# A diffusion backbone layer on one core: four staging tiles, branch tiles loaded in the output projection, late low parts, down-projection operands staged ahead, modulation weights in eight loads

## The chip, the cores and the metric

The kernel runs on one core of one Trainium2 chip. Each core has five engines that are programmed apart and meet by semaphores: TensorE (PE, with its weight loads shown as PEld), VectorE (DVE), ScalarE (ACT), GpSimd (POOL) and SyncE (SP), which here issues the transfers between the chip's main memory and the on-chip SBUF. Matrix products land in a second on-chip memory, PSUM. The metric is device time in microseconds of one execution. Lower is better.

## The reference

One layer over 2048 latent tokens of 1024 channels, with 256 context tokens ahead of them, all in 32-bit floats. What matters of it:

```python
mx = (silu(c) @ ada_w + ada_b).reshape(b, 1, 6, 1024)       # six modulation vectors
hx = rmsnorm(x, norm1_g) * (1 + mx[:, :, 1]) + mx[:, :, 0]
ux = hx @ w_in                                              # 1024 -> 5120
ox = hgrn_bidir(...)                                        # gated recurrence, 4 heads of 128
y_a = fourier_mix(ux[..., :512]) @ w_a                      # 2-D DFT over positions and channels
y_b = hgrn_readout(ux, ox) @ w_b
yx = (sigmoid(ux[..., GA]) * y_a + sigmoid(ux[..., GB]) * y_b) @ w_out
x = x + mx[:, :, 2] * yx
h2 = rmsnorm(x, norm2_g) * (1 + mx[:, :, 4]) + mx[:, :, 3]
z = depthwise_conv_3x3(h2 @ ffn_up) + ffn_conv_b            # 1024 -> 5632, grid of 32 x 64
x = x + mx[:, :, 5] * ((silu(z[..., :2816]) * z[..., 2816:]) @ ffn_down)
return rmsnorm(x, final_g)
```

## The kernel before

**Products in two parts.** An operand is split into a high part (`hi`, rounded to the format that the matrix product reads) and a low part (`lo = raw - hi`), and a product is three matmuls: hi x hi, hi x lo, lo x hi (`mm3`, L140). `load_split` (L105) loads a raw block of 128 x 512 into a staging tile `rw` (two of them per pool), ScalarE copies it to `hi` (L102), and GpSimd, or VectorE where it is named, subtracts for `lo` (L103). The staging tile is free after the subtraction.

**Order.** The program's text is not the order of issue. The build traces it, and a planner places each engine's instructions by dependences, tile slots and a model of times, with earlier text ahead where both are ready. `tc.issue_after(ins)` holds what is traced inside it behind `ins` on the engine of `ins`, without a wait for its end. Each engine, and SP's queue of transfers, then runs its list strictly in order.

**Stages, in order of time.** `startup` (L277) loads the first two modulation vectors' weights (`ada_w`, 1024 x 2048) as sixteen blocks of 128 x 1024, alternating halves, with the first tokens after the fifth block; it also loads six short vectors as rows (`vec_rows`, L258) on SP's queue, and the weights of the Fourier channels. The products of phase 1 follow: input projection, Fourier mix and recurrence.

Phase 2 (L840) goes over four blocks of 512 tokens. For each, `branches` (L862) loads eight branch tiles `y` (four of the Fourier branch, four of the recurrence) and goes over eight columns `j`: two weight blocks (`wab`), two gate tiles (`gt`, four slots), two products of twelve matmuls into `pj` (two slots), two gate products on VectorE (L895), their sum (L896), and the split into `mh` and `ml`. Between the columns it steps `bg`, a generator that normalizes, transposes and splits the previous block for the feed-forward part (`h2_block`, L934; for the third block `reload_steps`, L951, which reloads the block from memory piece by piece as `xc`). `out_proj` (L902) then multiplies by `w_out` in two halves `c` of 512 columns, eight steps `k` of twelve matmuls each.

Phase 3 (L977) makes 44 tiles of the up-projection `z`. For each, ScalarE applies the centre tap (L997) and the tap below (`be`, L999), VectorE the other seven (L1027), GpSimd adds `be` (L1003); each pair is gated (L1012) and stored to `dZ`.

`down` (L1030) makes eight groups `gi`: two column halves by four token blocks. A group is 22 steps `k` of twelve matmuls: operand `g` from `dZ`, weight `wd` from `ffn_down` (loaded in the groups 0 and 4, kept for the others). After each group four tiles are evicted: times the modulation `m5` (L1095), plus `x` (L1096), squares on ScalarE (L1098); in the second half the inverse root (`rsqrt`, L117), the scaling of a whole row of 1024 (L1107) and the store (L1108).

## Time and profile before

| | us |
|---|---|
| median of three runs | 3155.86 (3153.78 to 3157.29) |
| profiled execution, its own time | 3159.88 |
| its span, first to last instruction | 3158.1 |
| TensorE matmul busy | 3081.7 (98%) |
| TensorE weight load busy | 2556.2 (81%) |
| VectorE busy | 1742.6 (55%) |
| GpSimd busy | 949.1 (30%) |
| ScalarE busy | 930.7 (29%) |

The profile is that of one execution. The share of an engine is an average over stages with different limits, so the stages are read one by one. A matmul's recorded end is modelled, and successive matmuls overlap; the distance from start to start, that is, the length of a stretch over the count of its matmuls, says how fast they go. "PEclk" is the share of its full clock that TensorE was granted. Lines of the kernel are given as L and a number.

### The profile page before, as it was taken

The page shows a single profiled execution, that of the slowest core. Times are in us where ns is not written, and L with a number is a line of the kernel's source. Part 1 is how long each engine was busy: PE and PEld are TensorE (multiplying, and loading weights), DVE is VectorE, ACT ScalarE, POOL GpSimd, SP SyncE. Part 2 cuts the span into 40 slices and gives each one's busy share as a digit, 9 for nine tenths or more (in the row PEclk, how much of TensorE's full clock was granted, in tenths as well). Part 3 has the DMA queues.
Part 4 walks back from the last instruction along what each step waited for, and adds up shares of the span by engine and source line. Part 5 has one row for each costly group of instructions (what it writes and reads, how often), then busy time and mean ns, then how long its engine had stood idle before and what let it go on. Part 6 is the DMA issues. An engine that isn't in the chain of part 4 may idle for free.

```text
span 3158.1 us, 38963 instructions
## 1 busy us (share of the span) xinstructions
PE 3081.7 (98%) x14955; PEld 2556.2 (81%) x14955; DVE 1742.6 (55%) x2493; ACT 930.7 (29%) x1498; POOL 949.1 (30%) x563
## 2 busy tenths in 40 slices
PE   7999999999999999999999999999999998999998
PEld 4977788888888888777877888888888887788786
DVE  6355533566666640366665777777777777111324
ACT  4322111233333331233433222222222223223322
POOL 2200110000000010343443444344444345444543
PEclk9999999999999999999999999999999999999999
DMA  6255644433223232656552111111111113545643
GB/s 245 86 164 185 196 153 150 139 107 105 91 95 112 99 108 74 206 171 209 175 181 68 54 60 50 41 54 47 54 54 34 54 54 114 173 132 168 204 149 132
DMA packets 283051, 374.70 MB, mean 119 GB/s; under 512 B 20701, under 2 KB 158833, under 8 KB 279537
## 3 DMA queue, kind: packets, MB, share of 16 engines
q1 hardware_dynamic: 282865, 372.21, 36.0%
q8 instruction: 118, 1.93, 0.2%
q14 instruction: 68, 0.56, 0.1%
HBM read 270.68 MB, written 101.45 MB: 118 GB/s over the span
## 4 chain that ended last, share of the span: by engine, by line
PE 83%; DMA 6%; DVE 4%; POOL 2%; issue 2%; ACT 2%; SPq 0%; ACTq 0%; DVEq 0%; POOLq 0%
PE z L146 10%; PE z L144 10%; PE z L145 10%; PE pj L144 9%; PE pj L146 9%; PE pj L145 9%; PE dn L1079 4%; PE dn L1078 4%; PE dn L1077 4%; PE pa L782 4%; PE wo L925 1%; PE wo L926 1%; PE wo L924 1%; DMA rw<-in_ffn_down_dram 1%; PE kv L654 1%
## 5 line engine op out<-in xcount | busy, mean ns | idle before, releaser
L1027 DVE SCALAR_TENSOR_TENSOR ac<-z,cw,ac 128x1953 f32<-128x1953 f32 (+2 forms) x308 | 700.8, 2275 | 253.2 <-ACT be L999 242.1
L145 PE MATMUL z<-h,w_up 128*128 128x512 f32 x1408 | 548.0, 389 | 0.0
L146 PE MATMUL z<-h,w_up 128*128 128x512 f32 x1408 | 548.0, 389 | 0.0
L144 PE MATMUL z<-h,w_up 128*128 128x512 f32 x1408 | 547.9, 389 | 0.0
L1003 POOL TENSOR_TENSOR ac<-ac,be 128x1984 f32<-128x1984 f32 x44 | 196.8, 4472 | 427.1 <-DVE ac L1027 413.9
L103 POOL TENSOR_TENSOR gl<-rw,gh 128x512 fp32r<-128x512 f32 x176 | 233.0, 1327 | 274.5 <-ACT gh L102 265.5
L145 PEld LDWEIGHTS z<-h,w_up 128*128 128x128 f32 x1408 | 264.3, 188 | 54.9
L146 PEld LDWEIGHTS z<-h,w_up 128*128 128x128 f32 x1408 | 264.3, 188 | 54.8
L144 PEld LDWEIGHTS z<-h,w_up 128*128 128x128 f32 x1408 | 264.3, 188 | 54.6
L1079 PE MATMUL dn<-wd,gl 128*128 128x512 f32 x704 | 279.8, 397 | 6.2 <-POOL gl L103 5.9
L1077 PE MATMUL dn<-wd,gh 128*128 128x512 f32 x704 | 278.9, 396 | 6.0 <-ACT gh L102 5.8
L1078 PE MATMUL dn<-wd,gh 128*128 128x512 f32 x704 | 278.5, 396 | 0.0
L997 ACT ACTIVATE ac<-z,vt,cw 128x2048 f32<-128x2048 f32 x44 | 90.9, 2066 | 636.4 <-PE z L146 636.4
L102 ACT CAST gh<-rw 128x512 fp32r<-128x512 f32 x176 | 108.8, 620 | 304.2 <-PE dn L1078 206.8
L488 ACT ACTIVATE ev<-pj 128x512 f32<-128x512 f32 (+1 forms) x136 | 79.6, 585 | 367.0 <-PE pj L146 343.3
L1079 PEld LDWEIGHTS dn<-wd,gl 128*128 128x128 f32 x704 | 133.0, 189 | 41.2 <-POOL gl L103 10.4
L1077 PEld LDWEIGHTS dn<-wd,gh 128*128 128x128 f32 x704 | 133.2, 189 | 38.1 <-ACT gh L102 7.1
L1095 DVE TENSOR_TENSOR dtmp<-dn,m 128x512 f32<-128x512 f32 x32 | 21.4, 684 | 249.3 <-PE dn L1079 249.3
L1078 PEld LDWEIGHTS dn<-wd,gh 128*128 128x128 f32 x704 | 133.0, 189 | 31.1
L103 POOL TENSOR_TENSOR w_up<-rw,w_up 128x512 fp32r<-128x512 f32 x88 | 112.8, 1306 | 90.3 <-ACT w_up L102 90.3
L782 PEld LDWEIGHTS pa<-bQ,bkc 128*128 128x128 f32 x896 | 120.7, 191 | 17.0 <-issue 10.5
L782 PE MATMUL pa<-bQ,bkc 128*128 128x128 f32 x896 | 127.5, 286 | 1.3
(310 smaller groups left out, 6193.0 us busy)
## 6 DMA issues: line engine op xcount, KB each, us to landing
rw<-dZ SPq DMA_DIRECT2D x176, 256.0 KB, 3.0
rw<-in_ffn_up_dram SPq DMA_DIRECT2D x88, 256.0 KB, 3.4
dZ<-ac SPq DMA_DIRECT2D x22, 1024.0 KB, 4.4
rw<-in_w_in_dram SPq DMA_DIRECT2D x72, 256.0 KB, 3.2
maw<-in_ada_w_dram SPq DMA_DIRECT2D x64, 256.0 KB, 3.2
rw<-in_w_out_dram SPq DMA_DIRECT2D x64, 256.0 KB, 3.2
x<-dX SPq DMA_DIRECT2D x48, 256.0 KB, 4.9
rw<-in_ffn_down_dram SPq DMA_DIRECT2D x44, 256.0 KB, 3.2
```

Of the source, the lines that this page charges most:

```text
L102: self.nc.scalar.copy(hi, raw)
L103: (eng or self.nc.gpsimd).tensor_tensor(lo, raw, hi, op=SUB)
L144: self.nc.tensor.matmul(ps, lh, rh, start=start and i == 0, stop=False)
L145: self.nc.tensor.matmul(ps, lh, rl, start=False, stop=False)
L146: mm = self.nc.tensor.matmul(ps, ll, rh, start=False, stop=stop and i == last)
L782: mm = nc.tensor.matmul(pa[:, c], kc[:, c], fap(Q, w * P, [(2 * m, nw), (W + m, 2), (1, m)]), start=True, stop=True)
L997: nc.scalar.activation(ac, z, AF.Identity, scale=self.cw[:, 4, jj:jj + 1], bias=self.v("cb", jj))
L1003: nc.gpsimd.tensor_tensor(ac[:, :SEQ - 64], ac[:, :SEQ - 64], be[:, 64:], op=ADD)
L1027: nc.vector.scalar_tensor_tensor(o, z3[:, r0 + dy:r1 + dy, c0 + dx:c1 + dx], self.cw[:, k, jj:jj + 1], o, op0=MUL, op1=ADD)
L1077: nc.tensor.matmul(accs[i], gh[:, t], wh, start=(kk == 0), stop=False)
L1078: nc.tensor.matmul(accs[i], gh[:, t], wl, start=False, stop=False)
L1079: nc.tensor.matmul(accs[i], gl[:, t], wh, start=False, stop=(kk == NF - 1))
```

## The change

It has six parts.

1. Start-up: the modulation weights come as eight blocks of 128 x 2048, and the first tokens after the second of them. The six short vectors are loaded on GpSimd's queue, ahead of the weights, and transposed after the fourth block. The first half of the Fourier weights is split before the second is loaded.
2. Branch projections: the staging tiles of two pools are used in turn, two and two, for weights, branch tiles and output weights. The gate tiles have five slots. `ml` of a column is formed after the first gate product of the next column. The steps of `bg` are held behind the column's matmuls, and in the last block they are spread 0, 1, 1, 1, 1, 1, 1, 2.
3. The branch tiles of block n + 1 are traced in the second half of block n's output projection, one a step.
4. From phase 3 to `down`: on the last up-projection tile the tap below goes to VectorE as an eighth step, and `be` and GpSimd's addition are left out there. Ahead of the centre tap, all 22 weights of the first down half are loaded raw into free tiles, six of them are split, and three operands are loaded and split. Further operands of the first group come in fours into a tile of `be`. The eviction of group 0 is traced at step 3 of group 1.
5. Second half of `down`: `m5` is multiplied into the weights as they are loaded, in two staging tiles of their own; the eviction there is one addition. The first half is stored already times `final_g`, and ScalarE scales it at the end while VectorE scales the second half; they are stored apart. The last five steps, instead of four, go tile by tile.
6. `rsqrt` starts with one instruction instead of two.

The core of the diff:

```diff
-            nc.sync.dma_start(vr[r:r + n, :], ap.rearrange("o (r p) -> (o r) p", p=P))
+            nc.gpsimd.dma_start(vr[r:r + n, :], ap.rearrange("o (r p) -> (o r) p", p=P))
...
+            wt = wts[:, k % 2, :]
+            nc.sync.dma_start(wt, a["ada_w"][0, k * P:(k + 1) * P, :2 * D])
...
-        nc.vector.tensor_scalar(t.bitcast(I32), v.bitcast(I32), 1, None, op0=ALU.logical_shift_right)
-        nc.vector.tensor_scalar(y.bitcast(I32), t.bitcast(I32), -1.0, float(0x5F3759DF), op0=MUL, op1=ADD)
+        nc.vector.tensor_scalar(y.bitcast(I32), v.bitcast(I32), -0.5, float(0x5F3759DF), op0=MUL, op1=ADD)
...
-            gates[j] = [p4.tile([P, TB], F32, name=f"gt{b}", tag="gt", bufs=4) for b in range(2)]
+            gates[j] = [p4.tile([P, TB], F32, name=f"gt{b}", tag="gt", bufs=5) for b in range(2)]
...
-                self.load_split(hi[:, o, :], lo[:, o, :], wsrc[0, :, j * P:(j + 1) * P].rearrange("(k p) c -> p k c", p=P))
+                self.load_split(hi[:, o, :], lo[:, o, :], wsrc[0, :, j * P:(j + 1) * P].rearrange("(k p) c -> p k c", p=P),
+                                None, p4 if b else None)
...
                 nc.vector.tensor_tensor(gt, pj, gt, op=MUL)
+                if b == 0:
+                    low()
             nc.vector.tensor_tensor(gts[0], gts[0], gts[1], op=ADD)
-            self.split(mg_hi[:, j, :], mg_lo[:, j, :], gts[0], nc.vector)
-            for _ in range((0, 0, 1, 1, 1, 1, 2, 2)[j]):
-                next(bg, None)
+            nc.scalar.copy(mg_hi[:, j, :], gts[0])
+
+            def low(j=j, g=gts[0]):
+                nc.vector.tensor_tensor(mg_lo[:, j, :], g, mg_hi[:, j, :], op=SUB)
+
+            with self.tc.issue_after(mm.ins):
+                for _ in range(((0, 0, 1, 1, 1, 1, 2, 2) if n < 3 else (0, 1, 1, 1, 1, 1, 1, 2))[j]):
+                    next(bg, None)
...
+    def load_branch(self, p4, n, i):
+        y = p4.tile([P, 2, TB], F32R, name=f"y{n}{i}", tag="yo", bufs=8)
+        src = self.dY[i][:, n * TB:(n + 1) * TB] if i < 4 else self.dO[i - 4][n][:]
+        self.load_split(y[:, 0, :], y[:, 1, :], src, self.nc.vector, p4 if i % 2 == 0 else None)
...
+                if c and n + 1 < NB:
+                    self.load_branch(p4, n + 1, k)
...
+                end = jj == 2 * NF - 1
+                if end:
+                    self.wd, self.first = [], []
+                    self.load_raw()
+                    for k in range(6):
+                        self.load_wd(0, k)
+                        if k < 3:
+                            self.first.append(self.load_g(0, k))
+                self.centre = nc.scalar.activation(ac, z, AF.Identity, scale=self.cw[:, 4, jj:jj + 1], bias=self.v("cb", jj))
+                if not end:
+                    be = p5.tile([P, SEQ], F32, name="be", tag="be", bufs=2)
...
+    def load_wd(self, gi, k, times=None):
+        if gi == 0:
+            self.split(w[:, 0, :], w[:, 1, :], self.wraw[k], None if k < 8 else self.nc.vector)
+        else:
+            self.load_split(w[:, 0, :], w[:, 1, :], src[0, k * P:(k + 1) * P, cs], self.nc.vector, self.p6, 2, times, "wr")
...
+    def load_raw(self):
+        for pool, tag, n in ((self.pw, "w", 4), (self.ph, "H6", 8), (self.ph, "H7", 8), (self.pw, "w", 2)):
+            t = pool.tile([P, 8 if n == 8 else 4, TB], F32, name="wraw", tag=tag, bufs=1 if n == 8 else 2)
+            for i in range(0, n, 2):
+                k = len(self.wraw)
+                self.nc.sync.dma_start(t[:, i:i + 2, :], src[0, k * P:(k + 2) * P, :TB].rearrange("(k p) c -> p k c", p=P))
...
+    def load_g(self, gi, k):
+        early = gi == 0 or gi == 1 and k < 3
+        pool, nb = (self.pr, 3) if early else (self.p6, 5)
...
+                    with tc.issue_after(self.centre.ins):
+                        if tg == 0 and k >= (0 if c else 6):
+                            self.load_wd(gi, k, m5[:, cs] if c else None)
+                        if len(gs) == k:
+                            gs.append(self.first.pop(0) if gi == 0 and k < 3 else self.load_g(gi, k))
...
+                    rs = self.rsqrt(p6, vv, 1)
+                    nc.scalar.activation(xt[:, 0:TB], xt[:, 0:TB], AF.Copy, scale=rs)
+                    nc.sync.dma_start(self.out[ti * P:(ti + 1) * P, 0:TB], xt[:, 0:TB])
+                    nc.vector.scalar_tensor_tensor(x, x, rs, fg[:, cs], op0=MUL, op1=MUL)
+                    nc.sync.dma_start(self.out[ti * P:(ti + 1) * P, cs], x)
```

More of the change, by code (lines that the diff above doesn't have):

```diff
@@ L114, in load_split @@
         self.last_load = self.nc.sync.dma_start(t, src)
+        if times is not None:
+            self.nc.vector.tensor_tensor(t, t, times, op=MUL)
         self.split(hi, lo, t, eng)
@@ L166, in run @@
             self.phase2()
[L167 to L170 removed]
+            pr = tc.tile_pool(name="pr", bufs=1, reuse_waits="tile", side="right")
+            self.pr = pr.__enter__()
+            p5 = tc.tile_pool(name="p5", bufs=1, reuse_waits="tile")
+            self.p5 = p5.__enter__()
+            last = self.phase3(self.p5)
+            self.down(last, (p5, pw, pr))
             hpool.__exit__(None, None, None)
@@ new lines, in startup @@
+        turn = self.vec_rows(p0)
+        for k in range(KD):
+            if k % 2 == 0:
+                wts = self.ph.tile([P, 2, 2 * D], F32, name=f"adw{k}", tag=f"H{4 + k // 2}")
+            wt = wts[:, k % 2, :]
+            nc.sync.dma_start(wt, a["ada_w"][0, k * P:(k + 1) * P, :2 * D])
+            for n in (2, 3, 0, 1):
+                wc = wt[:, n * TB:(n + 1) * TB]
+                if n == 3:
+                    for w in range(2):
+                        cc = self.sc[:, w, k:k + 1]
+                        if k == 0:
+                            nc.vector.tensor_scalar(accv[w], wc, cc, None, op0=MUL)
+                        else:
+                            nc.vector.scalar_tensor_tensor(accv[w], wc, cc, accv[w], op0=MUL, op1=ADD)
+                else:
+                    mm = nc.tensor.matmul(accs[n][0:2, :], self.sc[:, :, k], wc, start=(k == 0), stop=(k == KD - 1))
+            if k == 3:
+                with self.tc.issue_after(mm.ins):
+                    turn()
+            if k == 1:
+                xs = self.load_x(p0, 0, [x0[:, i, :] for i in range(4)])
@@ L906, in out_proj @@
         mg_hi, mg_lo = mg
+        self.br = []
         for i in range(4):
@@ L1020, in conv @@
             for dx in (0, -1, 1):
-                if dx == 0 and dy >= 0:
+                if dx == 0 and (dy == 0 or dy > 0 and not below):
                     continue
@@ new lines, in load_g @@
+    def load_g(self, gi, k):
+        tg = gi % NB
+        early = gi == 0 or gi == 1 and k < 3
+        pool, nb = (self.pr, 3) if early else (self.p6, 5)
+        gh = pool.tile([P, TB], F32R, name="gh", tag="gh", bufs=nb)
+        gl = pool.tile([P, TB], F32R, name="gl", tag="gl", bufs=nb)
+        if early and (gi or k >= 3):
+            q = k if gi else (k - 3) % 4
+            if q == 0:
+                self.graw = self.p5.tile([P, 4, TB], F32, name="graw", tag="be", bufs=2)
+                for i in range(3 if gi else min(4, NF - k)):
+                    self.last_load = self.nc.sync.dma_start(self.graw[:, i, :], self.dZ[k + i][:, tg * TB:(tg + 1) * TB])
+            self.split(gh, gl, self.graw[:, q, :])
+        else:
+            self.load_split(gh, gl, self.dZ[k][:, tg * TB:(tg + 1) * TB], None, pool, 2 if early else 4)
+        return gh, gl
```

177 lines of the change are left out of this document (81 added, 96 removed).

## The prediction

> **What bounds the kernel now.** First the page: busy shares and the chain that ended last.
>
> ```profile
> PE 3081.7 (98%) x14955; PEld 2556.2 (81%) x14955; DVE 1742.6 (55%) x2493; ACT 930.7 (29%) x1498; POOL 949.1 (30%) x563
> ...
> PE 83%; DMA 6%; DVE 4%; POOL 2%; issue 2%; ACT 2%; SPq 0%; ACTq 0%; DVEq 0%; POOLq 0%
> ```
>
> TensorE is busy 98% of the span and carries 83% of the chain. The change removes no matmul, so it can win only where TensorE waits. The second view is busy time by stretch (length, then busy time and count of each engine, granted clock, DMA share, GB/s), cut at the stages.
>
> ```profile
> core 0: us, PE busy (x) PEld busy (x) DVE busy (x) ACT busy (x) POOL busy (x), PEclk, DMA share, GB/s
> 1285.00:1333.50 48.50, 43.83 (x191) 35.36 (x190) 26.25 (x32) 14.89 (x26) 21.49 (x15) 1.00 0.70 230
> 1333.50:1377.00 43.50, 43.50 (x193) 36.02 (x193) 19.31 (x27) 13.85 (x23) 12.31 (x9) 1.00 0.51 164
> 1377.00:1430.00 53.00, 50.37 (x231) 41.22 (x230) 42.30 (x63) 24.45 (x41) 29.04 (x21) 0.97 0.61 199
> 1473.70:1526.00 52.30, 49.54 (x227) 40.64 (x227) 41.97 (x62) 24.06 (x41) 28.94 (x21) 0.97 0.63 201
> 1570.00:1633.00 63.00, 55.89 (x245) 44.54 (x244) 45.60 (x68) 24.13 (x40) 29.38 (x21) 0.95 0.70 222
> 1700.00:2500.00 800.00, 800.00 (x3531) 662.43 (x3530) 584.40 (x257) 218.75 (x170) 341.78 (x131) 1.00 0.16 50
> 2636.80:2714.00 77.20, 65.61 (x266) 50.86 (x265) 36.25 (x22) 28.63 (x42) 42.04 (x26) 0.93 0.53 171
> 2720.00:2890.00 170.00, 170.00 (x733) 137.83 (x733) 12.47 (x19) 44.23 (x81) 77.87 (x60) 1.00 0.41 132
> 2940.00:3140.00 200.00, 200.00 (x859) 160.91 (x858) 66.46 (x202) 56.08 (x103) 96.57 (x73) 1.00 0.48 160
> 3145.40:3158.10 12.70, 0.22 (x1) 0.00 (x0) 8.70 (x40) 1.45 (x4) 0.00 (x0) 0.66 0.39 157
> ```
>
> The up-projection (1700 to 2500) has no hole: 800/3531 = 226.6 ns a matmul. The holes, counted as length less PE busy plus length times the missing clock: branch projections of block 0, 48.50 - 43.83 = 4.7 us; of block 1, 2.6 + 1.6 = 4.2; of block 2, 2.8 + 1.6 = 4.4; of block 3, 7.1 + 3.2 = 10.3; first group of the down-projection, 11.6 + 5.4 = 17.0; and 12.7 after the last matmul. Those 53 us and the start-up are the stake.
>
> Is the missing clock a cost of its own? Two stretches, inside a hole and behind it:
>
> ```profile
> 1390.80:1393.30 2.50, 0.26 (x2) 0.00 (x0) 2.50 (x5) 0.62 (x1) 0.00 (x0) 1.00 0.45 125
> 1394.80:1398.20 3.40, 3.40 (x11) 2.59 (x11) 1.96 (x4) 1.14 (x2) 1.27 (x1) 0.53 0.52 166
> ```
>
> A hole of 2.5 us is followed by 3.4 us at 0.53 of the clock: another 1.6 us. The Trainium skill, TensorE: Matmul & The Clock Gate, "Why this matters for your kernels", only asks for no idle gap above about 3 us, and by it this hole would have left the clock alone; the clock terms of blocks 1 and 2, 3.2 us, would not be there. The rows decide, and I count them.
>
> **The change part by part.** The terms are summed against the profiled execution's own 3159.88 us.
>
> (1) Start-up: modulation weights in eight loads, the six vector rows on POOL's queue.
>
> ```profile
> 15.82 0.29 SPq L266 DMA_DIRECT2D vr<-in_norm_g_dram  x1
> ...
> 23.53 3.08 SPq L318 DMA_DIRECT2D adw<-in_ada_w_dram  x5
> ```
>
> ```profile
> 20.00:22.00 2.00, 2.00 (x4) 0.39 (x3) 1.86 (x6) 0.00 (x0) 0.00 (x0) 0.50 1.04 414
> 22.00:30.00 8.00, 8.00 (x22) 1.79 (x21) 6.12 (x13) 0.06 (x1) 0.00 (x0) 0.95 0.77 244
> ```
>
> Six small loads hold SP from 15.82 to 23.53, 7.7 us, before the remaining weights are issued. Behind them the DMA falls from 414 to 244 GB/s for 8 us: 1.36 MB not moved, 3.3 us at 414. With the six on POOL, which is idle in both stretches, the last weight lands sooner and all that follows moves as a block. Against it, that last load is 1 MB instead of 512 KB, 1.3 us more at 414 GB/s. The ends are -7.7 (all of SP's time) and +1.3; I take **-3**, near the row of bytes. The Trainium skill, DMA: Bandwidth & Descriptors, "Issuing engines are not separate DMA queues", says that another issuing engine saves only the time to issue; by it, six times 0.29, the term would be -1.7.
>
> (2) Branch projections: four staging tiles, five gate tiles, late low parts, background steps queued behind the matmuls.
>
> ```profile
> PE pj L144 <- DVE gt L895: 10.0, 5, 2.8
> PE pt L435 <- DVE xc L966: 3.1, 2, 2.1
> ```
>
> ```profile
> 1288.74 3.12 DMA rw<-in_w_b_dram
> ...
> 1293.05 1.71 DVE ml L103
> 1294.78 0.33 SPq L873
> 1295.21 4.81 DMA rw<-in_w_a_dram
> ```
>
> ```profile
> L948 DVE TENSOR_SCALAR x<-x,rs_y 128x1024 f32<-128x1024 f32 x4 | 2.7, 750 | 0.0
> L126 DVE SCALAR_TENSOR_TENSOR rs_t<-rs_t,vv 128x4 f32<-128x4 f32 x3 | 1.6, 521 | 0.1
> ```
>
> Block 0 is a loop of loads: the weight load waits for its staging tile, ACT copies (0.62 us, as in the first clock row), VectorE forms the low part of the merged tile, only then may SP load the next gate (its tile comes free), and behind that stands the next weight load. Two staging tiles more let the weights be fetched a column ahead, and the low part stands behind the next gate product instead of ahead of it. TensorE needs 24 x 226.6 ns = 5.4 us a column, the trip of one load (3.1 to 4.8 + 0.6 + the low part) is about as long, so one column ahead covers it: **-4** of 4.7. What the deferral adds: a gate tile is held for half a column longer; the fifth tile pays for it.
>
> Blocks 1 and 2 wait for something else: the gate product at L895 stands in VectorE's queue behind the reciprocal root (L126, whose mean of 521 ns for 4 columns shows it held up) and four normalizations (L948, 2.7 us). That order stays; the root loses one instruction of about 0.2 us. I take **-1** of 8.6, ends -6 and +1.
>
> In block 3 TensorE stands in a transpose that waits for `xc` (3.1 us) while ready projections queue behind it. The change puts each step behind its column's matmuls and starts it a column earlier, one step a column, with `xc` two steps ahead. What is late next is the double step in column 7. **-7.5** of 10.3, ends -10 and -2. Moving the steps puts no new DMA on a queue.
>
> (3) Output projection: branch tiles of the next block.
>
> ```profile
> L103 DVE TENSOR_TENSOR y<-rw,y x7: 678/681/693, 1332.6 to 1349.6; 128x512 fp32r<-128x512 f32 x7
> ```
>
> They were split there already (1332.6 to 1349.6, first half of block 0's output projection), in a stretch where PE is busy 43.50 of 43.50. The change moves eight loads with their copies from the first half to the second, past SP's weight loads. Sixteen loads on four tiles in 96 x 226.6 ns = 21.8 us leave 5.4 us for a trip, and 3.1 + 0.6 + 0.7 is 4.4. **0**; ends 0 and +6 a block, three times, if the trip is 7 us.
>
> (4) From up- to down-projection.
>
> ```profile
> ACT wd L102 <- DMA rw<-in_ffn_down_dram: 24.1, 12, 2.6
> ...
> PE dn L1077 <- ACT gh L102: 5.8, 1, 5.8
> ```
>
> ```profile
> 2644.96 2.05 ACT L997 ACTIVATE ac<-z,vt,cw 128x2048 f32<-128x2048 f32 x1
> 2646.91 1.96 ACT L999 ACTIVATE be<-z,cw 128x2048 f32<-128x2048 f32 x1
> 2648.76 1.91 ACT L1001 ACTIVATE ac<-ac 128x2048 f32<-128x2048 f32 x1
> ```
>
> ACT waits 24.1 us for weight loads that two staging tiles feed; so the convolution's three activations start only at 2644.96, 8 us after the last up-projection matmul, and the next operand copy waits 5.9 us behind them (the 5.8 us hole). After the change raw weights wait in SBUF, six weights and three operands are split ahead, L999 is gone, and the two activations left, 4.0 us, lie beside three tiles of matmuls, 36 x 226.6 ns = 8.2 us. VectorE takes one convolution step more (2.3 us, no one waits: its result is needed 21 tiles, 57 us, after). Of 17.0 I leave 2 for the first trips of the later operands: **-15**, ends -17 and -8.
>
> (5) Down-projection, second half's weights. These go through two tiles of their own with a VectorE product between load and copy.
>
> ```profile
> 2909.03 4.44 DMA rw<-in_ffn_down_dram
> ```
>
> A trip is 4.4 + 0.7 + 0.6 + 0.7 = 6.4 us, 3.2 a weight on two tiles, against 12 x 232.8 ns (200/859) = 2.8 that TensorE takes. 22 weights fall 9 us behind, and a lead of five operand tiles covers 14. VectorE's burst at the change of group grows by a product and a small operation a tile, 4 x 0.9 = 3.6 us, which eats into that lead: **+2**, ends 0 and +9.
>
> (6) Tail.
>
> ```profile
> 3145.22 0.40 PE L1079 MATMUL dn<-wd,gl 128*128 128x512 f32 x1
> ```
>
> ```profile
> 3153.11 1.29 DVE L1107 SCALAR_TENSOR_TENSOR x<-x,rs_y,fg 128x1024 f32<-128x1024 f32 x1
> ```
>
> From 3145.6 on VectorE runs three L1107 of 1.29 us, which halve (ACT takes the other half): 1.8; one product of 0.7 goes, two small operations a tile, and the last store is half as large. **-4** of 12.7, ends -5 and -1.
>
> The sum: -3 - 4 - 1 - 7.5 + 0 - 15 + 2 - 4 = -32.5, so 3127.4 on the profiled execution. Its 3159.88 stands 4.0 above the median of the three runs, 3155.86; against that the forecast is **3123**.
>
> **The rivals.** (A) The down-projection also runs faster a matmul. It takes 170/733 = 231.9 and 200/859 = 232.8 ns where the up-projection takes 226.6, with no wait; its operands lie in a pool whose layout the change alters. 1848 matmuls behind the first group times 5.5 ns are 10: 3113. No row says what sets the 5 ns, so the other sign is as open. (B) The loads were early already, as the row of (3) shows for the branch tiles; then (2) gives a quarter: 3123 + 9 = 3132. (C) Slower: the second half of the output projection becomes bound by its loads. If a trip through the four tiles takes longer than 5.4 us, every 1 us costs 16/4 = 4 us a block, 12 in all; to eat 32.5 it must take 8.1 us. At 7 us the kernel ends at 3142, at 9 us at 3166. For it: 4.81 us of DMA alone above; VectorE and ACT also evict the first half there. Against: the first half carried the same loads with no hole, and a trip there adds up to 4.4. (D) The two tiles of (5) bind: 3123 + 8 = 3131.
>
> **How the numbers follow.** Forecast 0.52, A 0.12, B 0.17, D 0.09, C 0.10, of which 0.07 beyond 8.1 us a trip. The predicted time is the forecast's. The range 3105 to 3143 takes in A with half of (1)'s and (2)'s further ends below, and B with D above; C's far end is left out. Less than 0.2%, 6 us, is about what a measurement here cannot tell from no change. Faster by more: the forecast, A, B, D and the milder C, 0.90; same 0.03; slower 0.07.
>
> **What the new profile would show.** Steps right: the first matmuls of the down-projection in one run with the last of the up-projection, no ACT wait on its weights above a few us, clock 1.00 there; no PE wait on `xc`; block 0's projection stretch at 44 us; blocks 1 and 2 still with a hole of 2 to 3 us each; under 9 us behind the last matmul. Wrong: PE waits on `wo` or on branch tiles in the output projections, on `wd` in the fifth down group, or SP held before the first operand loads of the down-projection by the raw loads that wait for `H6` and `H7`.

## The result and the profile after

The changed kernel takes 3133.42 us (median, 3131.04 to 3134.18) against 3155.68 for the kernel before on the same chip: a ratio of 0.9928, 95% interval 0.9911 to 0.9946, 22.3 us less. Forecast was 3123, range 3105 to 3143. The profiled execution went from 3159.88 to 3133.75, 26.2 us less where the sum of terms said 32.5. So of the 10 us by which the time lies above the forecast, 6 are terms. The other 4 were taken off because the profiled execution of before stood 4.0 above its median; that of after stands only 0.3 above its own.

The page of the changed kernel, busy times and the chain that ended last:

```profile
PE 3075.3 (98%) x14955; PEld 2561.1 (82%) x14955; DVE 1750.7 (56%) x2475; ACT 935.8 (30%) x1513; POOL 963.4 (31%) x568
...
PE 91%; DVE 4%; DMA 2%; issue 1%; ACT 1%; POOL 1%; SPq 0%; DVEq 0%; ACTq 0%; POOLq 0%
```

TensorE carries 91% of the chain where it carried 83, and DMA 2% where it carried 6. Busy time by stretch, cut at the first matmul of each stage (length, busy time and count of each engine, granted clock, DMA share, GB/s):

```profile
core 0: us, PE busy (x) PEld busy (x) DVE busy (x) ACT busy (x) POOL busy (x), PEclk, DMA share, GB/s
1281.75:1325.25 43.50, 43.50 (x193) 36.05 (x192) 22.97 (x31) 13.96 (x24) 25.55 (x15) 1.00 0.74 246
...
1369.40:1421.15 51.75, 47.70 (x225) 39.06 (x224) 42.47 (x60) 23.09 (x39) 29.78 (x21) 1.00 0.64 205
...
1560.15:1614.85 54.70, 49.77 (x225) 40.28 (x224) 43.66 (x63) 23.12 (x39) 29.50 (x21) 0.97 0.76 238
...
2624.05:2689.35 65.30, 62.08 (x266) 50.55 (x264) 28.84 (x23) 25.99 (x42) 43.20 (x26) 0.97 0.45 162
2689.35:2754.70 65.35, 63.27 (x266) 50.77 (x265) 26.32 (x35) 21.38 (x41) 33.74 (x24) 0.97 0.57 185
2760.00:2930.00 170.00, 170.00 (x733) 138.00 (x732) 43.23 (x65) 51.46 (x95) 84.22 (x62) 1.00 0.48 158
...
3122.50:3131.90 9.40, 0.20 (x1) 0.00 (x0) 4.63 (x19) 2.17 (x4) 0.00 (x0) 0.74 0.42 159
```

The projections of block 0 have no hole left (43.50 of 43.50); those of blocks 1 and 3 still have 4.1 and 4.9 us, and the first two groups of the down-projection 3.2 and 2.1, with a clock of 0.97 in three of these stretches. What TensorE waits for in phase 2 (total, times, longest):

```profile
PE pj L146 <- DVE gt L899: 7.1, 4, 2.4
PE pt L441 <- issue: 2.3, 1, 2.3
PE pj L146 <- DVE rs_t L128: 2.0, 1, 2.0
PE pj L146 <- ACT wab L102: 1.7, 1, 1.7
```

and in the down-projection:

```profile
PE dn L1198 <- POOL gl L103: 4.3, 3, 2.8
PE dn L1196 <- ACT gh L102: 1.0, 1, 1.0
```

TensorE's wait of 5.8 us for the operand copy `gh` in group 0, which stood behind ScalarE's waits for the down weights, is gone. Of the waits for `xc` in block 3 one is left: the 2.3 us that the view above puts down to "issue" end 0.1 us behind the last `xc`, which VectorE forms in column 7.

```profile
1612.78 1.37 DVE L989 TENSOR_TENSOR xc<-xc,rs_y 128x512 f32<-128x512 f32 x1
...
1614.25 0.63 PE L441 MATMUL pt<-eye,xc 128*128 128x128 f32 x4 [2.26 <-issue]
```

Stage by stage, from the first matmul of a stage to the first of the next (worked out from the matmuls' start times in each trace; the last column but one is the time behind the last matmul, the last the ratio of all runs to the kernel before on the same chip):

| run | up to block 0 | projections 0, 1, 2, 3 | output projections 0, 1, 2, 3 | down groups 0, 1, then 2 to 7 | tail | ratio |
|---|---|---|---|---|---|---|
| before | 1284.8 | 49.0, 51.9, 51.8, 58.1 | 43.5, 44.8, 44.0, 45.3 | 77.0, 61.4, 61.4 to 62.6 | 12.7 | 1 |
| after | 1281.5 | 43.5, 51.8, 51.8, 54.7 | 44.2, 43.6, 43.6, 45.3 | 65.3, 65.3, 61.35 | 9.4 | 0.9928 |
| u1, two staging | 1282.9 | 48.9, 50.8, 50.6, 57.6 | 43.8, 44.5, 45.1, 47.7 | 65.3, 65.3, 61.35 | 10.0 | 0.9959 |
| u2, low at once | 1280.0 | 43.5, 53.4, 53.2, 55.7 | 44.4, 43.6, 43.6, 43.7 | 65.2, 65.5, 61.6 | 9.3 | 0.9923 |
| u3, old steps | 1278.0 | 43.5, 51.8, 53.3, 50.4 | 44.0, 44.2, 43.6, 44.1 | 65.2, 65.3, 61.35 | 9.4 | 0.9911 |
| u4, branch back | 1283.1 | 43.5, 56.2, 59.0, 57.4 | 45.3, 46.0, 45.9, 45.0 | 65.3, 65.3, 61.35 | 9.4 | 0.9967 |
| u5, rows on SP | 1286.1 | 43.5, 52.0, 53.4, 53.9 | 43.6, 43.6, 43.6, 45.3 | 63.6, 63.8, 61.35 | 8.9 | 0.9924 |
| p1, pad | 1280.7 | 43.5, 51.7, 51.8, 53.9 | 44.5, 43.7, 43.7, 45.2 | 63.6, 62.6, 59.84 | 9.6 | 0.9885 |
| d1, one dtmp | 1278.7 | 43.5, 52.4, 52.0, 51.4 | 44.1, 43.6, 43.6, 43.7 | 65.7, 61.2, 61.35 | 9.6 | 0.9903 |
| g1, low on POOL | 1278.5 | 43.5, 51.8, 52.1, 55.5 | 44.5, 43.7, 43.6, 43.7 | 73.6, 65.2, 61.35 | 9.4 | 0.9941 |
| c1 | 1278.2 | 43.5, 53.4, 53.4, 54.0 | 44.0, 43.6, 44.3, 45.0 | 61.0, 59.8, 59.84 (61.0 once) | 10.0 | 0.9861 |
| c2 | 1277.5 | 43.5, 49.9, 49.8, 54.0 | 43.6, 43.6, 43.7, 43.7 | 62.4, 59.8, 59.84 | 9.7 | 0.9839 |
| c3 | 1280.3 | 43.5, 53.4, 52.0, 51.9 | 44.4, 44.0, 43.6, 44.1 | 61.4, 59.8, 59.84 (60.9 once) | 9.6 | 0.9855 |
| c4 | 1279.4 | 43.5, 49.8, 49.9, 51.7 | 43.7, 43.8, 43.6, 44.1 | 60.6, 59.8, 59.84 | 9.9 | 0.9837 |

The up-projection, between the two blocks of columns, is 963.9 to 964.0 in all. The stage times of a row are those of one execution, and not always a middle one: u4's is the slowest of its seven (3155.26, median 3147.67), u3's and d1's are the fastest of their four (3126.75, median 3130.06; 3123.25, median 3128.35). After, p1, d1, g1 and c1 issue the whole of phases 1 and 2 in the same order, so they show how far a stage varies by itself: 1278.2 to 1281.5 up to block 0, 51.7 to 53.4 in blocks 1 and 2, 51.4 to 55.5 in block 3, not at all in block 0. Differences below that are not read.

Much of that variation is the clock. Behind a hole it may fall to half for 3.4 us, which costs 1.7; behind the same hole in another execution it stays. In block 1 the change and c1 have the same holes, 4.05 us in all, and the second of 2.4 us each. This is what follows it in the change, then in c1, and then the whole of block 1 in c1 (the change's row stands above: 51.75 us, clock 1.00):

```profile
1387.30:1390.70 3.40, 3.40 (x17) 2.86 (x18) 2.25 (x4) 0.97 (x2) 0.00 (x0) 1.00 0.48 156
...
1385.30:1388.70 3.40, 3.40 (x12) 2.72 (x11) 1.11 (x2) 0.58 (x2) 0.00 (x0) 0.50 0.61 154
...
1365.73:1419.10 53.37, 49.31 (x226) 40.24 (x224) 42.35 (x59) 22.90 (x39) 29.74 (x20) 0.97 0.63 196
```

So holes and clock are read apart below where it matters.

### The profile page after: what moved, and what is told of

Its sections match the earlier page's. It is cut to its first block, busy times and chain, and to the rows that moved or that the text cites. A ratio compares the mean times of both kernels' runs of the same rounds, so it can differ in the third digit from the quotient of the medians.

```text
span 3131.9 us, 38972 instructions
## 1 busy us (share of the span) xinstructions
PE 3075.3 (98%) x14955; PEld 2561.1 (82%) x14955; DVE 1750.7 (56%) x2475; ACT 935.8 (30%) x1513; POOL 963.4 (31%) x568
## 4 chain that ended last, share of the span: by engine, by line
PE 91%; DVE 4%; DMA 2%; issue 1%; ACT 1%; POOL 1%; SPq 0%; DVEq 0%; ACTq 0%; POOLq 0%
PE z L148 10%; PE z L147 10%; PE z L146 10%; PE pj L146 10%; PE pj L148 10%; PE pj L147 10%; PE dn L1198 5%; PE dn L1196 5%; PE dn L1197 5%; PE pa L788 4%; PE wo L946 2%; PE wo L947 2%; PE wo L945 2%; PE kv L660 1%; PE pj L379 1%
## 5 line engine op out<-in xcount | busy, mean ns | idle before, releaser
L147 PEld LDWEIGHTS z<-h,w_up 128*128 128x128 f32 x1408 | 264.4, 188 | 54.7
L148 PEld LDWEIGHTS z<-h,w_up 128*128 128x128 f32 x1408 | 264.4, 188 | 54.7
L103 POOL TENSOR_TENSOR gl<-rw,gh 128x512 fp32r<-128x512 f32 x154 | 207.2, 1353 | 233.6 <-ACT gh L102 213.6
L102 ACT CAST gh<-rw 128x512 fp32r<-128x512 f32 x154 | 94.4, 618 | 245.6 <-PE dn L1197 179.1
L103 POOL TENSOR_TENSOR wab<-rw,wab 128x512 fp32r<-128x512 f32 x64 | 93.5, 1480 | 110.4 <-ACT wab L102 110.4
```

What stands on the lines that cost most here:

```text
L102: self.nc.scalar.copy(hi, raw)
L103: (eng or self.nc.gpsimd).tensor_tensor(lo, raw, hi, op=SUB)
L147: self.nc.tensor.matmul(ps, lh, rl, start=False, stop=False)
L148: mm = self.nc.tensor.matmul(ps, ll, rh, start=False, stop=stop and i == last)
```

## The experiments: phase 2 taken apart

Four kernels undo one part each of the changed kernel. The fifth gate tile, the raw weights ahead of the down-projection (the largest gain) and parts 5 and 6 were not undone; what is said of them is read from the two traces.

**u1.** Two staging tiles per user.

```diff
-                                None, p4 if b else None)
+                                None, None)
...
-        self.load_split(y[:, 0, :], y[:, 1, :], src, self.nc.vector, p4 if i % 2 == 0 else None)
+        self.load_split(y[:, 0, :], y[:, 1, :], src, self.nc.vector, p4)
...
-                                p4 if q else None)
+                                None)
```

> The changed kernel with two staging tiles again for each user in phase 2 (branch weights and output weights all through the first pool's pair, branch tiles all through the second pool's pair); late low parts, five gate tiles, the held steps and all else stay. Theory (the prediction's): block 0's projections are a loop of loads, and the two more staging tiles are what opens it. Then block 0's projections go back from 43.5 us to 48 to 49, block 3's rise by 1 to 2, the output projections by 0 to 1 each: 3139 to 3142 us against 3133.4. Rival: the low part that no longer stands ahead of the next gate load is what opened the loop; then block 0 stays within 1 us of 43.5 and the kernel at 3133 to 3135.

Measured: 0.9959 (0.9944 to 0.9974) of the kernel before. Its projections of block 0:

```profile
1283.10:1332.05 48.95, 45.99 (x194) 36.89 (x192) 24.25 (x32) 14.99 (x26) 22.04 (x15) 0.97 0.68 221
```

That is the length of before, 49.0, but not made of the same: holes of 3.0 us and 1.7 of clock, where before had 4.7 of holes at full clock. Without the two tiles block 0's gain is gone; some 1.7 us of its holes stay closed by the other parts. Block 3, at 57.6, lies above what the change's order shows (51.4 to 55.5) and near the 58.1 of before. The output projections 1 to 3 are 0.9 to 2.4 us longer too, which the expectation put at 0 to 1.

**u2.** The low part of the merged tile at once.

```diff
-            nc.scalar.copy(mg_hi[:, j, :], gts[0])
-            def low(j=j, g=gts[0]):
-                nc.vector.tensor_tensor(mg_lo[:, j, :], g, mg_hi[:, j, :], op=SUB)
+            self.split(mg_hi[:, j, :], mg_lo[:, j, :], gts[0], nc.vector)
```

> The changed kernel with the low part of the merged tile formed at once, behind its high part, as before; four staging tiles, five gate tiles and the held steps stay. Theory (the prediction's): with weights a column ahead the low part in VectorE's queue is covered; block 0's projections stay within 1.5 us of 43.5, blocks 1 to 3 rise by 0 to 1 each: 3133 to 3137 us. Rival (the low part's place was the opener): block 0 goes back to 47 to 49 us and the others rise by 1 to 2 each: 3139 to 3143.

Measured: 0.9923 (0.9909 to 0.9938), not to be told from the change itself. Block 0 stays at 43.5. Blocks 1 and 2 show 53.4 and 53.2 us, which the change's order shows by itself too (c1).

**u3.** The background steps as before.

```diff
-            with self.tc.issue_after(mm.ins):
-                for _ in range(((0, 0, 1, 1, 1, 1, 2, 2) if n < 3 else (0, 1, 1, 1, 1, 1, 1, 2))[j]):
-                    next(bg, None)
+            for _ in range((0, 0, 1, 1, 1, 1, 2, 2)[j]):
+                next(bg, None)
```

> The changed kernel with the background steps between the columns as before: not held behind the column's matmuls, and 0, 0, 1, 1, 1, 1, 2, 2 in block 3 too. Theory (the prediction's): only block 3 answers, where TensorE waits again in a transpose for xc (3.1 us of waits); its projections go from 54.7 back to 57 to 58 us, blocks 1 and 2 stay within 0.5 of 51.8: 3136 to 3137 us. Rival: block 3's gain of 3.4 us came from the staging tiles and the late low parts; then it stays within 1 us of 54.7 and the kernel at 3133 to 3134.

Measured: 0.9911 (0.9895 to 0.9928), with an interval that overlaps the change's. The theory fell, in the direction that neither side had: in this trace block 3 is shorter than in any of the change's order.

```profile
1558.50:1608.90 50.40, 47.60 (x222) 38.61 (x220) 44.06 (x62) 22.73 (x39) 29.41 (x20) 1.00 0.77 237
```

Its hole is 2.8 us where the change has 4.9, the clock 1.00 where the change has 0.97, and of the 2.3 us for which a transpose waited for the last `xc` this is left:

```profile
PE pt L441 <- issue: 0.3, 1, 0.3
```

With the old steps the last four transposes come behind the first matmul of the output projection (222 matmuls in the row, 225 in the change's), so block 3 and its output projection are compared together: 94.5 us against 100.0.

**u4.** The branch tiles at the start of each block.

```diff
-                if c and n + 1 < NB:
-                    self.load_branch(p4, n + 1, k)
...
             for n in range(NB):
+                for i in range(KD):
+                    self.load_branch(p4, n, i)
                 mg = self.branches(...)
```

> The changed kernel with the branch tiles of each block traced at the start of that block's projections, as before, and not in the second half of the output projection. Theory (the prediction's term of 0): the loads were early already, and the move is worth nothing; every stage stays within 0.6 us and the kernel at 3132 to 3135 us. Rival: the move keeps them out of the way of the gate and weight loads at a block's start; without it blocks 1 to 3 rise by 1 to 2 us each, 3137 to 3140.

Measured: 0.9967 (0.9956 to 0.9978), 0.0039 or 12 us slower than the change, far beyond the rival's 4 to 7. Its trace is of the slowest of seven executions, 7.6 us above their median, so its stages and waits show where the time goes and overstate how much. Its waits in phase 2:

```profile
PE pj L148 <- POOL wab L103: 7.3, 4, 2.1
PE pj L146 <- ACT wab L102: 5.8, 3, 2.2
PE pj L146 <- DVE gt L899: 5.6, 2, 2.8
```

In it TensorE waits 13.1 us for branch weights, where the change has 1.7 and the kernel before 1.4. The staging tiles are taken in turn by weights and branch tiles, and traced together at a block's start they stand in each other's way.

## The experiments: the start

**u5.** The six short vectors on SP's queue.

```diff
-            nc.gpsimd.dma_start(vr[r:r + n, :], ap.rearrange("o (r p) -> (o r) p", p=P))
+            nc.sync.dma_start(vr[r:r + n, :], ap.rearrange("o (r p) -> (o r) p", p=P))
```

> The changed kernel with the six short vectors loaded on SP's queue again, at the same place of the text, ahead of the eight weight loads. Theory (the prediction's row of bytes): the six loads hold SP and the weights behind them, and taking them off SP is what gave the 3.2 us at the start; the first products come 2 to 3.5 us later and the kernel ends at 3136 to 3137 us. Rival (six times 0.29 us of issue each, as the row of one such load says): 1.5 to 2 us, 3135. Second rival: the gain came from the eight larger loads, and the place of the six is worth under 0.5 us.

Measured: 0.9924 (0.9909 to 0.9939), no difference in time. The issues of the weights and the matmuls that use them (durations in ns, then first and last start), first in the kernel before, then in the change, then in u5:

```profile
L328 PE MATMUL ada<-adw,sc x48: 592/592/1061, 5.6 to 39.0; 128*2 128x512 f32 x48
L318 SPq DMA_DIRECT2D adw<-in_ada_w_dram x16: 328/354/462, 1.9 to 26.2; - x16
```

```profile
L334 PE MATMUL ada<-adw,sc x48: 592/592/1061, 7.1 to 34.9; 128*2 128x512 f32 x48
...
L323 SPq DMA_DIRECT2D adw<-in_ada_w_dram x8: 328/344/460, 1.9 to 12.2; - x8
```

```profile
L334 PE MATMUL ada<-adw,sc x48: 592/592/1061, 9.1 to 36.8; 128*2 128x512 f32 x48
...
L323 SPq DMA_DIRECT2D adw<-in_ada_w_dram x8: 328/344/484, 4.0 to 14.1; - x8
```

The last of these matmuls starts 4.1 us earlier in the change, 1.9 of it because the six are not on SP, 2.2 for the rest of the part (fewer, larger loads, and the six not in their midst). So the second rival is wrong in the trace, and the first is the nearest: six issues put the weights back by 2.1 us (1.9 to 4.0). The Trainium skill, DMA: Bandwidth & Descriptors, "Issuing engines are not separate DMA queues", says that another issuing engine saves the time to issue; with the six ahead of the weights the trace agrees. In the midst of the weights, as before, they cost more than their issue: from 22 to 30 us the DMA then moved 244 GB/s. The change moves 409:

```profile
22.00:30.00 8.00, 8.00 (x20) 1.54 (x19) 6.91 (x18) 0.30 (x2) 0.00 (x0) 1.00 1.01 409
```

How much of the 4 us is left at block 0 cannot be read, since that point varies by 3 us by itself. In u5's trace it comes at 1286.1, 4.6 us behind the change and outside of that variation, while the median time is the same; whether that is the 2 us and the clock, or more, is open.

## The experiments: the down-projection

**p1.** One small tile of the pool made 128 bytes larger.

```diff
-                        ss = p6.tile([P, 2, 16], F32, name="ss")
+                        ss = p6.tile([P, 4, 16], F32, name="ss")
```

> The changed kernel with one small tile of the down-projection's pool made 128 bytes larger, so that the operands gh and gl of that pool move by 128 bytes; nothing else changes. From step 3 of group 1 on the matmuls of the down-projection stand 232.4 ns apart, before it 226.7. In that first part gh and gl lie in another pool, at addresses that leave the remainder 224 on division by 256, as all the other large operands do; from step 3 of group 1 they leave 96. Theory: the place of the stationary operand against the moving one sets the 5.7 ns; with the pad all of the 1800 matmuls behind go to 226.7 ns, which is 10.3 us: 3122 to 3124 us. Rival (something else of that stage, for example its transfers or the queue of waits): the spacing stays at 232.4 and the kernel at 3133.

The places of the operands in a partition of SBUF, from the two programs (the order of instructions on every engine is the same in both):

```
                              after                  p1
weights wd (moving)           19936, rest 224        19936, rest 224     (rest on division by 256)
gh, gl up to group 1, step 2  212960, rest 224       212960, rest 224
gh, gl from group 1, step 3   159328, rest 96        159456, rest 224
```

Measured: 0.9885 (0.9870 to 0.9900), about 13.6 us less than the change. The stretch that took 733 matmuls in 170 us:

```profile
2760.00:2930.00 170.00, 170.00 (x751) 140.76 (x750) 44.67 (x66) 52.99 (x100) 85.54 (x64) 1.00 0.49 157
```

170/751 = 226.4 ns, and a group takes 59.84 us, 264 x 226.7 ns, against 61.35. The theory held: 1.51 us in each of six groups and 1.3 in the rest of group 1 are the 10.3 us expected. The other 3 lie where a run varies by itself (up to block 0, and the clock behind the holes of groups 0 and 1). The kernel before agrees: its first operands lie at 212960 too, and from group 1 on they lie at 188000 and behind (rest 96) and take 232.6 ns. Three things stay open. The pad moves every tile behind `ss`, also those that other engines read. Whether it is the place of the one operand against the other or the remainder 224 by itself was not tried (and not all operands of the kernel lie at 224, as the expectation says; some of phase 1 do not). And u2, with the same places as the change, takes 233.3 ns where the change takes 232.5, so something else is worth 0.8.

**d1.** One eviction tile.

```diff
-                        tmp = p6.tile([P, TB], F32, name="dtmp", tag="dtmp", bufs=2)
+                        tmp = p6.tile([P, TB], F32, name="dtmp", tag="dtmp", bufs=1)
```

> The changed kernel with one eviction tile dtmp instead of two. In group 1 the first eviction's second product starts at 2697.1 us, when the third operand tile of the old pool, which lies where the second dtmp comes to lie, is read for the last time; ScalarE's squares wait for it, and behind them in its queue the copy for step 4, for which TensorE waits (1.2 and 1.2 us, and a low clock behind). Theory: with one dtmp, which does not reach into that tile, the eviction starts some 6 us earlier and group 1 goes from 65.3 to 61.5 us; 3129 to 3130 us. Rival: the eviction of group 0 is late because its x tiles and m5 land late; then group 1 stays at 65 us and the kernel at 3133.

The changed kernel, VectorE and then ScalarE in order of time (start, length; in brackets the idle time before and what ended it):

```profile
2689.38 0.69 DVE L1128 TENSOR_TENSOR dtmp<-dn,m 128x512 f32<-128x512 f32 x1 [32.66 <-PE dn L1198]
2697.32 0.69 DVE L1128 TENSOR_TENSOR dtmp<-dn,m 128x512 f32<-128x512 f32 x1 [7.26 <-PE dn L1197]
```

```profile
2698.65 0.63 ACT L1130 ACTIVATE junk<-x 128x512 bf16<-128x512 f32 x1 [8.37 <-DVE x L1129]
```

The second product's wait was ended by a matmul of the down-projection, not by a load: the second dtmp begins at 212576 of a partition, 2048 bytes long, the old pool's first operand tile at 212960, and step 2 of group 1 reads that one last. With one tile, group 1:

```profile
2682.60:2743.75 61.15, 61.15 (x265) 49.72 (x264) 27.97 (x34) 21.65 (x40) 33.69 (x24) 1.00 0.62 198
```

Measured: 0.9903 (0.9888 to 0.9917). Group 1 lost its holes, 65.3 to 61.2 us, as expected; 1.7 of these 4.2 us are the clock behind the holes. The 0.0025 or 7.9 us in all, with intervals that overlap, is more than 4.2, and what is over lies where a run varies by itself (up to block 0, block 3).

**g1.** All low parts of the first half's weights on GpSimd.

```diff
-            self.split(w[:, 0, :], w[:, 1, :], self.wraw[k], None if k < 8 else self.nc.vector)
+            self.split(w[:, 0, :], w[:, 1, :], self.wraw[k], None)
```

> The changed kernel with the low parts of all 22 weights of the first down-projection half on GpSimd; in the changed kernel those from the ninth on are on VectorE. In group 0 one GpSimd subtraction takes 8.04 us (2649.6 to 2657.6) while VectorE runs eight subtractions of 0.68 us and the gate product back to back, and TensorE waits 2.8 us for it. Theory: VectorE's run shuts GpSimd out; without it no GpSimd operation of that stretch takes over 2 us, the hole goes, and group 0 falls from 65.3 to 61 to 62 us: 3129 to 3130 us. Rival: GpSimd has too much to do; 14 more subtractions of 1.3 us (18 us) make it late, and group 0 grows by 3 us or more.

The changed kernel, GpSimd and then VectorE:

```profile
2649.80 8.04 POOL L103 TENSOR_TENSOR gl<-graw,gh 128x512 fp32r<-128x512 f32 x1 [1.10 <-ACT gh L102]
```

```profile
2649.63 1.88 DVE L103 TENSOR_TENSOR wd<-wraw,wd 128x512 fp32r<-128x512 f32 x3
2651.43 2.28 DVE L1046 TENSOR_TENSOR ac<-ac 128x2048 f32<-128x2048 f32 x1
2653.64 3.08 DVE L103 TENSOR_TENSOR wd<-wraw,wd 128x512 fp32r<-128x512 f32 x5
```

Measured: 0.9941 (0.9925 to 0.9958), 4 us slower than the change, with intervals that overlap. In g1 GpSimd's subtractions (min, median, max in ns):

```profile
L103 POOL TENSOR_TENSOR gl<-graw,gh x22: 1272/1291/3202, 2627.5 to 2695.1; 128x512 fp32r<-128x512 f32 x22
L103 POOL TENSOR_TENSOR wd<-wraw,wd x18: 1272/1302/1339, 2623.8 to 2652.4; 128x512 fp32r<-128x512 f32 x18
```

and, in order of time, and as TensorE's wait:

```profile
2644.96 5.00 POOL L103 TENSOR_TENSOR wd<-wraw,wd 128x512 fp32r<-128x512 f32 x4
```

```profile
PE dn L1198 <- POOL gl L103: 9.4, 5, 3.2
```

The cause was right and the cure wrong. Nothing takes 8 us any more (3.2 at most, 1.29 in the median), but four `wd`, 5 us, stand ahead of one `gl` in GpSimd's queue, TensorE waits 9.4 us for `gl` instead of 4.3, and group 0 takes 73.6 us.

## The experiments: together

**c1** takes p1 and d1, and cures group 0 the other way, with the late operands' low parts on VectorE. **c2** adds the normalizations on ScalarE, **c3** adds the old steps of u3, **c4** both.

```diff
-            self.split(gh, gl, self.graw[:, q, :])
+            self.split(gh, gl, self.graw[:, q, :], self.nc.vector if gi == 0 and k >= 10 else None)
...
-            nc.vector.tensor_scalar(xs[i], xs[i], rs[:, i:i + 1], None, op0=MUL)
+            nc.scalar.activation(xs[i], xs[i], AF.Copy, scale=rs[:, i:i + 1])
```

> The changed kernel with three edits: the pad of 128 bytes in the down-projection's pool, one dtmp, and in group 0 the low parts of the operands from the eleventh on (k of 10 and more) on VectorE, between its own low parts, and not on GpSimd. Theory: the three act in different places and add: groups 1 to 7 at 59.9 us each, and in group 0 GpSimd has nothing left that VectorE's run could shut out, so that the 2.8 us wait for gl and the low clock behind it go (group 0 from 65.3, or 63.6 in two of the runs, to 60 to 61.5 us): the whole of the groups 420 to 422 us against 494.7 - 13.6, and 3113 to 3116 us. Rival: VectorE's queue then makes TensorE wait for gl instead, as GpSimd's did with 14 more subtractions; group 0 stays over 64 us, and the kernel at 3118 or more.

Measured: 3115.51 us, 0.9861 (0.9844 to 0.9877). Group 0:

```profile
2623.35:2684.30 60.95, 60.14 (x265) 49.49 (x264) 36.69 (x35) 25.84 (x42) 21.14 (x14) 1.00 0.50 175
```

The eight groups add up to 481.0 us: 61.0, six at 59.84, and one at 61.0 (the expectation's "420 to 422" left out a group and does not add up; by its own parts it was 479 to 481). TensorE's wait for `gl` in group 0 is down to 0.8 us, and no subtraction on GpSimd takes over 1.8 us there.

> The kernel of c1 with the four normalizations of a block's rows (0.75 us each, between the inverse root and the steps; blocks 0, 1 and 3) on ScalarE, with the inverse root as its scale, and not on VectorE. Theory: in blocks 1 and 2 the second hole (2.5 us) is the gate product that stands behind these four in VectorE's queue, and the first (1.8 us) is the root itself, held up by GpSimd; so the second goes and the first stays: projections of blocks 1 and 2 from 51.8 to 48.5 to 49.5 us, 5 to 7 us less than c1. Rival: ScalarE's copies for the branch weights (0.6 us each, two a half column) come to stand behind four activations of about 1.1 us, TensorE waits for wab, and the blocks stay at 51 to 53 us, no gain over c1.

Measured: 3106.24 us, 0.9839 (0.9824 to 0.9855), 9 us under c1, with intervals that overlap a little. The length of block 1, and the waits of phase 2:

```profile
1364.55:1414.45 49.90, 47.79 (x225) 38.99 (x224) 38.66 (x55) 26.83 (x43) 29.70 (x20) 1.00 0.67 213
```

```profile
PE pj L146 <- DVE rs_t L127: 3.4, 2, 1.7
PE pj L146 <- DVE rs_t L128: 2.1, 1, 2.1
PE pt L441 <- ACT wo L102: 1.1, 1, 1.1
```

The hole behind the normalizations is gone; the one at the root, 1.7 us a block, stays. What holds the root is seen in the changed kernel's block 1, VectorE and then GpSimd:

```profile
1377.38 0.16 DVE L127 TENSOR_TENSOR rs_t<-rs_y 128x4 f32<-128x4 f32 x1
1377.58 1.26 DVE L128 SCALAR_TENSOR_TENSOR rs_t<-rs_t,vv 128x4 f32<-128x4 f32 x1
1378.88 1.21 DVE L129 SCALAR_TENSOR_TENSOR rs_y<-rs_t,rs_y 128x4 f32<-128x4 f32 x1
```

```profile
1377.53 2.54 POOL L103 TENSOR_TENSOR wab<-rw,wab 128x512 fp32r<-128x512 f32 x2 [4.40 <-ACT wab L102]
```

Operations of 0.16 us last as long as the subtractions that GpSimd has begun. Blocks 1 and 2 are 49.8 to 49.9, a little above the expected 48.5 to 49.5, against 51.7 to 53.4 in all runs with the normalizations on VectorE and the branch tiles ahead, u1 excepted. Their holes went from 4.1 us each in c1 to 2.1; the rest of the difference to c1 is the clock, which fell in both blocks there and in neither here.

> The kernel of c1 with the background steps as in the kernel before (not held behind the column's matmuls, 0, 0, 1, 1, 1, 1, 2, 2 in each block). In the first such run block 3's projections took 50.4 us against 54.7 and no transpose waited on its queue. Theory: with four staging tiles and the late low parts the wait for xc is gone by itself, and holding the steps only makes the double step of column 7 a hole (0.9 to 2.4 us and a low clock behind): block 3 at 50 to 51.5 us, against 51.4 to 55.5 in the runs with held steps, 2 to 4 us less than c1 in the median of the times. Rival: block 3 varies by some 4 us from run to run whatever the steps; then c3 is within 1.5 us of c1.

Measured: 3113.53 us, 0.9855 (0.9840 to 0.9870), 2 us under c1 with overlapping intervals; its block 3, at 51.9, is a little above the expected 50 to 51.5.

> The kernel of c1 with both: normalizations on ScalarE and the old steps. If both theories hold, the gains add: blocks 1 and 2 at 48.5 to 49.5 us, block 3 at 50 to 51.5, 7 to 11 us less than c1, about 3105 us. If the normalizations on ScalarE only trade one wait for another, it equals c3; if the steps do not matter, it equals c2.

Measured: 3106.34 us, 0.9837 (0.9822 to 0.9852), as c2. In the traces block 3 takes 50.4, 51.9 and 51.7 us with old steps and 51.4 to 55.5 with held ones (seven runs, 53.9 in the mean, u1, u2 and u4 not counted); in the times of c2 and c4 that gain does not show. Together with the output projection behind it, as compared at u3, it is 94.5, 96.0 and 95.8 us against 95.0 to 100.0 (98.4 in the mean). The holes of block 3, without the clock, are 2.6 to 2.8 us with old steps and 2.9 to 5.6 with held ones. That held steps cost something in block 3 is likely, its size is open. c2 and c4 are the fastest kernels here, 1.6% under the kernel before, and both beat the change.

## Why the prediction was right, and where it was not

The time lay in the range, 10 us above the forecast, for the main reason given: TensorE's holes were the stake, and the largest gain is where it was forecast. But two terms, (4) and (5), came out beyond their own ends, to opposite sides, and that of blocks 1 and 2 is right by luck. Against the profiled execution, term by term:

| term | predicted | measured |
|---|---|---|
| (1) start-up | -3 | -3.2 up to block 0 (-3.2 to -6.6 in the same order) |
| (2) block 0 | -4 | -5.5 |
| (2) blocks 1 and 2 | -1 | -0.1 (holes +2.8, clock -3.4) |
| (2) block 3 | -7.5 | -3.4 |
| (3) output projections | 0 | -1.0 |
| (4) up- to down-projection | -15 | -11.7 in group 0, +4.0 in group 1 |
| (5) second half | +2 | -2.0 in groups 4 to 7 |
| (6) tail | -4 | -3.3 |
| sum | -32.5 | -26.2 |

- **(4) is the step that was mis-sized, by 7 us; its 7.7 lie outside of its ends, 8 to 17.** I left 2 us "for the first trips of the later operands". Group 0 kept holes of 3.2 us and 1.7 of clock, and neither was a trip of an operand: the largest, 2.8 us, was GpSimd shut out for 8.04 us. GpSimd was a second cause already before, in the same view as the wait for `gh`, and the sum left it out:

```profile
PE dn L1079 <- POOL gl L103: 5.3, 4, 3.1
```

Of these 5.3 us 4.3 are left, in groups 0 and 1. And the prediction gave no price to the eviction of group 0 that is traced at step 3 of group 1, though the change named it: it cost 4.0 us there, by the place of a tile of 2 KB (d1 gives back 4.2, of which 1.7 is the clock).

- **Block 3: the gain went to the wrong part.** I charged 7.5 us to the moved steps. u3 shows that the waits for `xc` go without them, all but 0.3 us, and u1 points to the staging tiles (57.6 with two). The view of before gave 3.1 us of these waits; 2.5 more, put down to "issue" there, also end 0.1 us behind an `xc`. What the prediction named as late next, the double step of column 7, was there as the 2.3 us wait of a transpose for `xc`; priced within the 2.8 us left, it came with a second hole that I had not counted, the root of the rows ahead of the gate product (2.0 us), to 6.5 us with the clock.
- **Block 0: right, with the part named.** Four staging tiles opened the loop (u1: 5.4 us back, of them 1.7 by the clock); the late low part is not needed for it (u2). The 0.8 us above the hole of 4.7 are what my way of counting hid: the window was 0.5 us shorter than the stage (48.50 against 49.0), and a matmul behind a gap counts longer as busy (191 at 226.7 ns are 43.3 us, the row says 43.83).
- **Blocks 1 and 2: right as a number, by luck.** The hole at the gate product stayed, and c2 shows that the four normalizations stand ahead of it, as the prediction said. But a second hole of 1.7 us came ahead of it, at the root: before, GpSimd formed the two low parts of a column's weights one by one there, and with four staging tiles it forms them back to back, 2.54 us, in which two steps of the root are stretched (read from the two traces; no run takes it apart). With two staging tiles (u1) the holes add up to 2.9 to 3.1 us, with four to 4.05, before to 2.6 to 2.8. The length stayed because the clock, which fell behind each hole before, did not fall in this execution; in c1, where it fell, the blocks take 53.4.
- **(3): right as a sum, wrong as an account.** The stretch is 1 us shorter, but "0" for the move hides that it is needed: without it (u4) the change loses 12 us of its 22. Four tiles that are shared in turn need loads that are traced apart.
- **(5): no wait came.** The fear of 3.2 us a weight against 2.8 did not show: group 4 is 1.2 us shorter than before and TensorE waits for no `wd` in it. The other 0.8 are pace, 232.5 ns a matmul for 233.3 before, without a cause shown. Rival D is out.
- **(6): right,** 12.65 to 9.36 us.
- **Rival A** did not happen, yet it was the largest gain at hand. The row for it was 232 ns beside 226.6, and I wrote that no row says what sets the 5 ns. A count by steps would have pointed there: group 0 ran at 226.7 in both kernels, group 4, which loads weights as group 0 does, at 233.3 before, so the change of pace came with the change of pool, not of load.
- **Rival B** gave 3132, near the time by another road: block 0's loads were not early, its 5.5 us came in full. **Rival C:** the output projections became shorter, not longer.
- **The clock** costs what the prediction's rows said where it falls, but it does not always fall. Behind the hole of group 0 (2654.7 to 2657.6) the change shows

```profile
2654.70:2657.60 2.90, 0.44 (x2) 0.02 (x1) 2.02 (x4) 0.46 (x1) 2.90 (x1) 1.00 0.78 319
...
2659.50:2662.70 3.20, 3.20 (x9) 2.49 (x8) 0.00 (x0) 0.62 (x1) 1.93 (x2) 0.50 0.00 0
```

3.2 us at half the clock, 1.6 us more for a hole of under 3. In p1 and u5 the same hole of 2.8 us has no low clock behind it, and group 0 takes 63.6 us for 65.3. The prediction counted the low clock as a sure part of each hole; it should have stood in the ends of the range.
- **The signs:** block 0 came as named (43.5 us), and the first down-projection follows the last up-projection without a hole. Others did not: ScalarE waits 14.8 us for the fifth of the weights (2609.9 to 2624.7, which TensorE does not feel), one wait for `xc` is left, blocks 1 and 2 have 4.1 us of holes instead of 2 to 3, and 9.4 us are left behind the last matmul instead of under 9.
- **Two slips in the working:** half of three times 1.29 us is 1.9, not 1.8; and with the milder C the chances of faster are 0.93, so that with 0.07 for slower nothing is left for the same.

## What to carry to other kernels

When loads of several kinds share staging tiles, look at which are traced together: the shared tiles opened block 0 here, and lost time in the later blocks until the branch loads were traced elsewhere. Count holes and low clock apart before two executions are compared: the same hole may or may not bring 1.7 us of low clock. Before a stage is called bound by matmuls, divide its length by their count and compare with the best stage; 2.5% of a stage was lost to the place of a tile here, and 128 bytes gave back 10 us beside the 22 of the whole change. When an operation moves late, ask whose place its tile takes, and what stands behind the wait on each engine.

## What the runs showed of the hardware

- Two matmul operands, the same instructions in the same order: 232.4 ns a matmul with the stationary operand at a remainder of 96 bytes (modulo 256) beside a moving one at 224, 226.7 with both at 224. The Trainium skill, SBUF — State Buffer, "Who interferes with whom", gives TensorE two independent read ports, one for the moving operand and one for weight loads, that wait for no one. No contention that it lists would set the 5.7 ns; p1 measured that 128 bytes of place do.
- A GpSimd subtraction, 1.29 us in the median, took 8.04 us beside nine VectorE instructions with two SBUF inputs, and ended 1.1 us behind the last of them (2657.8 and 2656.7). The Trainium skill, SBUF — State Buffer, "Who interferes with whom", says that such a VectorE instruction contends with a GpSimd instruction that reads SBUF, for a port pair that is an exclusive lock. The trace agrees, and shows more: GpSimd did not get in between the nine.
- The opposite way too: behind a block's rows, steps of VectorE's root on 4 columns took 1.2 us instead of 0.16 while GpSimd subtracted, and with them stood the gate product that TensorE waited for.
- The granted clock fell to 0.50 for 3.4 us behind a hole of 2.4 us in c1's block 1, and stayed at 1.00 behind the same hole in the change.
